# Last down projection: the remainders of the ordinary weight tiles are made by an adding DMA instead of VectorE

## The chip, the core and the metric

The kernel runs on one core of one Trainium2 chip. A core has TensorE (PE, the matrix products), VectorE (DVE, elementwise work), ScalarE (ACT, elementwise work and casts), GpSimd (POOL), SyncE (SP, which here issues the DMAs) and 16 DMA engines that move data between DRAM and the on-chip memory. Each engine works through its own queue in a fixed order and waits at semaphores. The metric is device time in microseconds (us). Before the change the median of three runs is 1831.31 us (1829.83 to 1831.4).

## What is computed

The reference is one transformer block on 256 tokens of width 2048, in float32: a feed-forward half step, a mixer (differential attention beside a causal convolution), and a second feed-forward half step, each with a normalisation, a modulation and a gated residual.

```
x = x + 0.5 * g1 * swiglu(h, ffn1_w_gu, ffn1_w_down)
x = x + gm * hybrid_mixer(h, ...)
x = x + 0.5 * g2 * swiglu(h, ffn2_w_gu, ffn2_w_down)
def swiglu(h, w_gu, w_down):
    g, u = split(h @ w_gu)          # 2048 -> 2 x 5632
    return (silu(g) * u) @ w_down   # 5632 -> 2048
```

The change lies in the very last product, `(silu(g) * u) @ ffn2_w_down`: 256 tokens by 5632 by 2048.

## The kernel before

Float32 accuracy is reached with three products of a faster, rounded type (fp32r). Every operand is split into a rounded part `hi` and a remainder `lo = value - hi`, and `mm3` (L326) adds `a_hi*w_hi` (L329), `a_hi*w_lo` (L333) and `a_lo*w_hi` (L334) into one PSUM accumulator.

Weights come from DRAM in tiles of 1 MB: 128 partitions by 4 pieces of 512 columns. `w_tile` (L288) loads a tile into a `raw` buffer with a DMA that SP issues (L294). Then, for each half of two pieces, ScalarE casts the half into a `whi` buffer (L305) and VectorE subtracts this from `raw` into a `wlo` buffer (L307). The pools are small: `rawp`, `whp` and `wlp` have four buffers each (L89 to L91). A `raw` buffer holds a whole tile, a `whi` or `wlo` buffer half a tile, so that two tiles' halves fit.

The last projection is `down_strassen` (L465). It goes twice (`np_` 0 and 1) over the 22 weight tiles `c` of one half of the output columns. Some tiles, listed in `SEVENS` (L57), are done with seven products in place of eight: tiles 3, 5, 9, 11, 13, 15, 17 in the first pass and 1, 3, 5 and so on to 17 in the second. I call these seven-product tiles. Each of them takes one `raw` buffer (loaded at L542), and is split by a helper (L512 on ScalarE, L513 on VectorE) into `b11`, `b21`/`b22`, `t1`/`t3` and `t4`/`t2`, four `whi` and four `wlo` buffers; sums of its pieces are made on VectorE in between (L547, L549, L550). It issues 7 * 3 = 21 products.

All other tiles are ordinary: they go through `w_tile` at L595 and issue 8 * 3 = 24 products, two token halves by two column halves by two contraction pieces. There are 15 of them in the first pass and 13 in the second, 28 in all. The last two of the second pass (20 and 21) are held: their products come at the very end, one accumulator after the other (L597, and the loop whose inner line is L630), so that each accumulator can be finished and stored while the next is still being summed.

Buffers are shared in order. A tile's cast can start only when the engine that last used that `whi` buffer is done with it, and here that is TensorE, some four half tiles earlier. The order of instructions on each engine's queue was fixed by a planner at build time; a blocked instruction blocks what is behind it on its own engine.

Of the kernel before, what the change touches and what calls it, by code (L numbers as in the profile page):

```python
# [16 lines left out]
F32 = mybir.dt.float32  # L17
F32R = mybir.dt.float32r
# [4 lines left out]
ALU = mybir.AluOpType  # L23
AX = mybir.AxisListType

P = 128
# [56 lines left out]
def block_kernel(ctx: ExitStack, tc: tile.TileContext, x_in, pos_in, w_ada, small, w_gu1, w_dn1,  # L83
                 w_in, w_out, w_gu2, w_dn2, out):
    nc = tc.nc
# [3 lines left out]
    rawp = ctx.enter_context(tc.tile_pool(name="rawp", bufs=4))  # L89
    whp = ctx.enter_context(tc.tile_pool(name="whp", bufs=4))  # L90
# [9 lines left out]
    def nm(s):  # L100
        uid[0] += 1
        return f"{s}_{uid[0]}"

    def blk(shape, dtype=F32):
        return blkp.tile(shape, dtype, tag="blk", name=nm("blk"))
# [7 lines left out]
    def acc_tile(shape=(P, 512)):  # L113
        return accp.tile(list(shape), F32, tag="acc", name=nm("acc"))

    def tp_tile(shape=(P, 512)):
        return tpp.tile(list(shape), F32, tag="tp", name=nm("tp"))
# [26 lines left out]
    for i in range(4):  # L144
        pc = acc_tile()
        for j in range(4):
            k = 4 * i + j
# [138 lines left out]
    w_dma = [None]  # L286

    def w_tile(src, held=False, ks=(0, 4), small_raw=False):  # L288

        k0, n = ks[0], ks[1] - ks[0]  # L290
        src = src.rearrange("p (k n) -> p k n", k=4)
        if not small_raw:
            raw = rawp.tile([P, 4, 512], F32, tag="raw", name=nm("raw"))
            w_dma[0] = nc.sync.dma_start(out=raw[:, :n, :], in_=src[:, k0:k0 + n, :])  # L294
        views = {}
        for h in range(0, n, 2):
            m = min(2, n - h)
            if small_raw:
                part = blk([P, 2, 512])
                w_dma[0] = nc.sync.dma_start(out=part[:, :m, :], in_=src[:, k0 + h:k0 + h + m, :])  # L300
                rw = part[:, :m, :]
            else:
                rw = raw[:, h:h + m, :]
            hi = blk([P, 2, 512], F32R) if held else whp.tile([P, 2, 512], F32R, tag="whi", name=nm("whi"))
            nc.scalar.copy(out=hi[:, :m, :], in_=rw)  # L305
            lo = blk([P, 2, 512], F32R) if held else wlp.tile([P, 2, 512], F32R, tag="wlo", name=nm("wlo"))
            nc.vector.tensor_sub(out=lo[:, :m, :], in0=rw, in1=hi[:, :m, :].bitcast(F32))  # L307
            for j in range(m):
                views[k0 + h + j] = (hi[:, j, :], lo[:, j, :])
        return lambda j: views[j]  # L310

    def w_first(cs, held):

        n = len(cs)
        raw = blk([P, 2, 512])
        w_dma[0] = nc.sync.dma_start(out=raw[:, :n, :], in_=w_gu1[cs[0]:cs[0] + n, 0].rearrange("c p n -> p c n")[:, :, :512])
        hi = blk([P, 2, 512], F32R) if held else whp.tile([P, 2, 512], F32R, tag="whi", name=nm("whi"))
        lo = blk([P, 2, 512], F32R) if held else wlp.tile([P, 2, 512], F32R, tag="wlo", name=nm("wlo"))

        def split():  # L320
            nc.scalar.copy(out=hi[:, :n, :], in_=raw[:, :n, :])  # L321
            nc.vector.tensor_sub(out=lo[:, :n, :], in0=raw[:, :n, :], in1=hi[:, :n, :].bitcast(F32))

        return [lambda j, i=i: (hi[:, i, :], lo[:, i, :]) for i in range(n)], split

    def mm3(acc, a, w, start, stop, lo_last=False):  # L326
        ah, al = a
        wh, wl = w
        nc.tensor.matmul(acc, ah, wh, start=start, stop=False)  # L329
        if lo_last:  # L330
            nc.tensor.matmul(acc, al, wh, start=False, stop=False)
            return nc.tensor.matmul(acc, ah, wl, start=False, stop=stop)
        nc.tensor.matmul(acc, ah, wl, start=False, stop=False)  # L333
        return nc.tensor.matmul(acc, al, wh, start=False, stop=stop)  # L334
# [130 lines left out]
    def down_strassen(w_dn, aT, a_act, gate_of, evac_last, share, pend, finish):  # L465
# [43 lines left out]
        def split(src, n):  # L509
            hi = whp.tile([P, 2, 512], F32R, tag="whi", name=nm("whi"))  # L510
            lo = wlp.tile([P, 2, 512], F32R, tag="wlo", name=nm("wlo"))
            nc.scalar.copy(out=hi[:, :n, :], in_=src)  # L512
            nc.vector.tensor_sub(out=lo[:, :n, :], in0=src, in1=hi[:, :n, :].bitcast(F32))  # L513
            return [(hi[:, i, :], lo[:, i, :]) for i in range(n)]
# [4 lines left out]
        for np_ in range(2):  # L519
# [17 lines left out]
            for c in range(NCH):  # L537
                share()
                first, last = c == 0, c == NCH - 1
                if c in SEVENS[np_]:  # L540
                    raw = rawp.tile([P, 4, 512], F32, tag="raw", name=nm("raw"))
                    nc.sync.dma_start(out=raw, in_=w_dn[np_, c].rearrange("p (k n) -> p k n", k=4))  # L542
                    s1, s2, s3, s4 = sums_of(c)
                    (b11,) = split(raw[:, 0:1, :], 1)
                    b21, b22 = split(raw[:, 2:4, :], 2)

                    nc.vector.tensor_sub(out=raw[:, 0:2, :], in0=raw[:, 1:4:2, :], in1=raw[:, 0:2, :])  # L547
                    t1, t3 = split(raw[:, 0:2, :], 2)
                    nc.vector.tensor_sub(out=raw[:, 3, :], in0=raw[:, 3, :], in1=raw[:, 0, :])  # L549
                    nc.vector.tensor_sub(out=raw[:, 2, :], in0=raw[:, 2, :], in1=raw[:, 3, :])  # L550
                    t4, t2 = split(raw[:, 2:4, :], 2)
                    go, end = c == SEVENS[np_][0], c == SEVENS[np_][-1]
                    if go:
                        if np_ == 0:
                            seven = [acc_tile(), acc_tile(), tp_tile(), tp_tile()]
                        else:
                            seven = [acc_tile() for _ in range(4)]
                    mm3(seven[0], a_act(2 * c, 0), b11, go, end)
                    mm3(plain[0], a_act(2 * c + 1, 0), b21, False, False)
                    mm3(plain[1], s4, b22, False, False)  # L560
                    mm3(seven[1], s1, t1, go, end)
                    mm3(seven[3], s3, t3, go, end)
                    mm3(seven[2], s2, t2, go, end)
                    mm3(plain[2], a_act(2 * c + 1, 1), t4, False, False)
                    tick()
                    if end:

                        p1, p5, p6, p7 = seven
                        u = [tmp([P, 512]) for _ in range(5)]
                        last_pair = np_ == 1  # L570
                        nc.scalar.copy(out=u[0], in_=p1)
                        nc.vector.tensor_add(out=u[4], in0=p6, in1=u[0])

                        def step_1(u=u, p5=p5):
                            nc.vector.tensor_add(out=u[1], in0=p5, in1=u[4])

                        def step_2(u=u, p7=p7):
                            nc.vector.tensor_add(out=u[2], in0=p7, in1=u[4])

                        def step_3(u=u, p5=p5):  # L580
                            nc.vector.tensor_add(out=u[3], in0=p5, in1=u[2])

                        def add(i, u=u):

                            t, n, xs = place(i)
                            nc.vector.tensor_mul(out=u[i], in0=u[i], in1=gbc[n])
                            nc.vector.tensor_add(out=xs, in0=xs, in1=u[i])

                        if last_pair:
                            todo += [lambda: (step_1(), add(0), add(1)), lambda: (step_2(), step_3(), add(2)),  # L590
                                     lambda: add(3)]
                        else:
                            todo += [step_1, step_2, step_3]
                    continue
                w = w_tile(w_dn[np_, c])  # L595
                if np_ == 1 and c >= NCH - 2:
                    held.append((c, w))  # L597
                    if todo:
                        todo.pop(0)()
                    continue  # L600
                for k in range(2):
                    for i, (t, n) in enumerate(order):
                        mm3(plain[i], a_act(2 * c + k, t), w(2 * k + n), first and k == 0, last and k == 1)
                tick()
                if first and np_ == 0:
                    while pend:
                        finish(*pend.pop(0))
                    gbc = gate_of()
                if todo:
                    todo.pop(0)()  # L610
# [691 lines left out]
    for ci in range(10):  # L1302
        p0 = 1 if ci < HOLD else 0
        accs = first[ci][2] if ci < HOLD else [acc_tile() for _ in range(NT)]
        for pc in range(p0, 4):
# [3 lines left out]
            w = w_tile(w_in[ci, pc], ci == 0 and pc <= PRE)  # L1309
# [52 lines left out]
    for i, (n, pc) in enumerate([(n, pc) for pc in range(4) for n in range(3)]):  # L1362
        w = w_tile(w_out[n, pc])
# [106 lines left out]
```

## Time and profile before

| | |
|---|---|
| median of three runs | 1831.31 us |
| the profiled execution's own time | 1830.85 us |
| its span, first to last instruction | 1829.0 us |
| TensorE busy, share of the span | 98% |
| VectorE busy | 84% |
| ScalarE busy | 55% |
| GpSimd busy | 2% |
| mean DMA traffic | 274 GB/s |

The profile is one execution. A row of a timeline gives the start in us from the beginning of the span, the duration in us, the engine, the line of the kernel, the operation, what it writes and reads, a count where equal rows are merged, and in brackets the idle time before it with what ended it. A row of a group gives the count, the total busy time, the mean of one in ns, and the idle time ahead of it. A windows row gives, for one stretch, the busy time and instruction count of PE, weight loading, DVE, ACT and POOL. The last projection runs from about 1580 us to the end at 1829.0 us.

### The profile page before, as it was taken

How to read it: one execution, taken by the hardware profiler on the slowest of the kernel's cores; microseconds unless marked ns; L12 is line 12 of the kernel's file. 1: busy time of each engine (PE TensorE's matmuls, PEld its weight loads, DVE VectorE, ACT ScalarE, POOL GpSimd, SP SyncE). 2: the span in 40 equal slices, each digit the busy share in tenths (PEclk: the TensorE clock that was granted, in tenths of full speed). 3: DMA queues.
4: the chain of work that ended last, by engine and by line, in shares of the span. 5: the costliest groups of instructions: out<-in, count | busy, mean ns of one | idle time of the engine just before them, and what ended most of it. 6: DMA issues, size and time to landing. Idle time of an engine off the chain costs nothing.

```text
span 1829.0 us, 21917 instructions
## 1 busy us (share of the span) xinstructions
PE 1800.7 (98%) x8111; PEld 1480.9 (81%) x8111; DVE 1531.0 (84%) x2040; ACT 1010.5 (55%) x1527; POOL 28.3 (2%) x29
## 2 busy tenths in 40 slices
PE   6999999999999999999999999999999999999998
PEld 5788888888888887788888787888888888878787
DVE  7889869999888787898999778878887865599897
ACT  7554344444444343566798655664755665555453
POOL 0000000000000000000110100000000000000000
PEclk9999999999999999999999999999999999999999
DMA  9987978889889998775544466889898966655552
GB/s 375 359 308 296 349 276 300 336 314 339 338 325 352 352 340 331 285 262 198 184 142 158 174 240 254 324 338 347 278 300 289 328 232 202 218 200 221 184 213 110
DMA packets 95962, 501.68 MB, mean 274 GB/s; under 512 B 31424, under 2 KB 31856, under 8 KB 38384
## 3 DMA queue, kind: packets, MB, share of 16 engines
q1 hardware_dynamic: 95856, 500.30, 74.7%
q8 instruction: 63, 1.03, 0.2%
q14 instruction: 43, 0.35, 0.1%
HBM read 492.37 MB, written 2.12 MB: 270 GB/s over the span
## 4 chain that ended last, share of the span: by engine, by line
PE 85%; DVE 8%; DMA 3%; ACT 3%; issue 2%; POOL 0%; SPq 0%; POOLq 0%; DVEq 0%; ACTq 0%
PE acc L333 27%; PE acc L334 27%; PE acc L329 27%; DVE wlo L307 2%; DVE wlo L513 1%; DMA raw<-in_w_ada_dram 1%; ACT whi L305 1%; DMA blk<-in_w_gu_dram 1%; PE acc L1137 1%; DVE raw L193 1%; DMA tmp<-tmp 1%; DVE blk L1029 1%; PE tp L851 1%; PE tp L333 1%; PE tp L334 1%
## 5 line engine op out<-in xcount | busy, mean ns | idle before, releaser
L333 PE MATMUL acc<-wlo,blk 128*128 128x512 f32 x2336 | 911.8, 390 | 6.3 <-DVE wlo L307 6.3
L329 PE MATMUL acc<-whi,blk 128*128 128x512 f32 x2339 | 909.5, 392 | 2.3 <-ACT blk L403 1.3
L334 PE MATMUL acc<-whi,blk 128*128 128x512 f32 x2336 | 910.7, 390 | 0.0
L305 ACT CAST whi<-raw 128x1024 fp32r<-128x1024 f32 (+1 forms) x577 | 592.4, 1044 | 475.5 <-PE acc L334 328.3
L307 DVE TENSOR_TENSOR wlo<-raw,whi 128x1024 fp32r<-128x1024 f32 (+1 forms) x577 | 686.5, 1210 | 180.3 <-ACT whi L305 179.5
L333 PEld LDWEIGHTS acc<-wlo,blk 128*128 128x128 f32 x2336 | 438.8, 188 | 101.4 <-DVE wlo L307 11.3
L329 PEld LDWEIGHTS acc<-whi,blk 128*128 128x128 f32 x2339 | 438.8, 188 | 94.6 <-ACT whi L305 2.7
L334 PEld LDWEIGHTS acc<-whi,blk 128*128 128x128 f32 x2336 | 438.5, 188 | 91.5 <-DVE blk L405 0.6
L193 DVE CUSTOM_DVE_ANT_0 raw<-raw,c_bc 128x2048 f32<-128x2048 f32 x142 | 324.2, 2285 | 10.3 <-DMA raw<-in_w_ada_dram 10.1
L512 ACT CAST whi<-raw 128x512 fp32r<-128x512 f32 (+1 forms) x64 | 60.5, 946 | 78.2 <-PE acc L334 27.5
L513 DVE TENSOR_TENSOR wlo<-raw,whi 128x512 fp32r<-128x512 f32 (+1 forms) x64 | 69.2, 1086 | 11.6 <-ACT whi L512 11.5
L666 ACT COPY blk<-acc 128x512 f32<-128x512 f32 x72 | 41.9, 589 | 62.6 <-PE acc L334 60.0
L1029 DVE SCALAR_TENSOR_TENSOR blk<-blk,cst,blk 128x245 f32<-128x245 f32 (+21 forms) x176 | 70.4, 455 | 0.6 <-ACT blk L1027 0.5
L830 DVE TENSOR_TENSOR blk<-acc,blk 128x512 f32<-128x512 f32 x88 | 56.7, 682 | 0.1
L845 ACT COPY tmp<-tmp 128x1024 uint16<-128x1024 uint16 x22 | 29.8, 1355 | 45.6 <-DMA tmp<-tmp 45.6
L831 ACT ACTIVATE blk<-blk 128x256 f32<-128x256 f32 x88 | 33.7, 413 | 19.6 <-DVE blk L830 19.4
L329 PE MATMUL acc<-blk,blk 128*128 128x512 f32 x104 | 40.8, 396 | 1.4 <-ACT blk L321 1.4
L333 PE MATMUL acc<-blk,blk 128*128 128x512 f32 x100 | 39.1, 391 | 0.8 <-DVE blk L307 0.8
L334 PE MATMUL acc<-blk,blk 128*128 128x512 f32 x100 | 39.0, 392 | 0.0
L351 DVE TENSOR_TENSOR blk<-tmp,blk 128x512 fp32r<-128x512 f32 x22 | 15.1, 688 | 22.3 <-ACT blk L350 22.3
L832 DVE TENSOR_TENSOR blk<-blk 128x256 f32<-128x256 f32 x88 | 33.8, 417 | 0.0
L307 DVE TENSOR_TENSOR blk<-raw,blk 128x1024 fp32r<-128x1024 f32 x24 | 28.9, 1220 | 2.0 <-ACT blk L305 2.0
(227 smaller groups left out, 1064.4 us busy)
## 6 DMA issues: line engine op xcount, KB each, us to landing
raw<-in_w_gu_dram SPq DMA_DIRECT2D x161, 1024.0 KB, 6.1
raw<-in_w_ada_dram SPq DMA_DIRECT2D x142, 1024.0 KB, 6.7
raw<-in_w_dn_dram SPq DMA_DIRECT2D x88, 1024.0 KB, 5.3
raw<-in_w_in_dram SPq DMA_DIRECT2D x40, 1024.0 KB, 4.8
raw<-in_w_out_dram SPq DMA_DIRECT2D x16, 1024.0 KB, 4.8
raw<-in_w_gu_dram SPq DMA_DIRECT2D x8, 768.0 KB, 6.3
blk<-in_w_gu_dram SPq DMA_DIRECT2D x10, 512.0 KB, 13.7
blk<-gate_line SPq DMA_DIRECT2D x6, 512.0 KB, 4.8
```

What stands on the lines that cost most here:

```text
L193: nc.vector.tensor_tensor_reduce(out=raw, in0=raw, in1=c_bc, scale=1.0, scalar=0.0, op0=ALU.mult, op1=ALU.add, accum_out=ada_cols[g][:, j ...
L305: nc.scalar.copy(out=hi[:, :m, :], in_=rw)
L307: nc.vector.tensor_sub(out=lo[:, :m, :], in0=rw, in1=hi[:, :m, :].bitcast(F32))
L329: nc.tensor.matmul(acc, ah, wh, start=start, stop=False)
L333: nc.tensor.matmul(acc, ah, wl, start=False, stop=False)
L334: return nc.tensor.matmul(acc, al, wh, start=False, stop=stop)
L512: nc.scalar.copy(out=hi[:, :n, :], in_=src)
L513: nc.vector.tensor_sub(out=lo[:, :n, :], in0=src, in1=hi[:, :n, :].bitcast(F32))
L666: last_part[0] = nc.scalar.copy(out=parts[c][:, t, :], in_=accs[t])
L830: nc.vector.tensor_add(out=p[:, t, :], in0=accs[t], in1=p[:, t, :])
L832: nc.vector.tensor_mul(out=p[:, t, 256:], in0=p[:, t, :256], in1=p[:, t, 256:])
L1029: nc.vector.scalar_tensor_tensor(out=y[:, d:], in0=u, scalar=w, in1=y[:, d:], op0=ALU.mult, op1=ALU.add)
```

## The change

The ordinary tiles of the last projection go through a new function, `w_tile_dma`, in place of `w_tile`. It loads the tile into `raw` and casts the halves into `whi` as before. VectorE's subtraction is gone. In its place ScalarE multiplies each rounded half by -1 and writes it into a tile `lo`. When both halves are there, a DMA issued by GpSimd reads the same 1 MB of weight from DRAM a second time and adds it onto `lo`, which leaves `weight - hi`. `lo` is not a `wlo` buffer: it is a whole tile from the pool `rawp`, with the tag `raw`, so it takes one of the four `raw` buffers until the tile's last product.

```diff
+    def w_tile_dma(src):
+
+        src = src.rearrange("p (k n) -> p k n", k=4)
+        raw = rawp.tile([P, 4, 512], F32, tag="raw", name=nm("raw"))
+        w_dma[0] = nc.sync.dma_start(out=raw, in_=src)
+        views = {}
+        lo = rawp.tile([P, 4, 512], F32R, tag="raw", name=nm("raw"))
+        for h in range(0, 4, 2):
+            hi = whp.tile([P, 2, 512], F32R, tag="whi", name=nm("whi"))
+            nc.scalar.copy(out=hi, in_=raw[:, h:h + 2, :])
+            nc.scalar.mul(lo[:, h:h + 2, :], hi.bitcast(F32), -1.0)
+            for j in range(2):
+                views[h + j] = (hi[:, j, :], lo[:, h + j, :])
+        nc.gpsimd.dma_start(out=lo, in_=src, accum_op=ALU.add)
+        return lambda j: views[j]
@@
-                w = w_tile(w_dn[np_, c])
+                w = w_tile_dma(w_dn[np_, c])
```

## The prediction

> **What bounds the kernel now.** I read the page's busy times first, then the stage of the change by windows, then who waits for whom there, and last the timeline of one pair of tiles. The page:
>
> ```profile
> span 1829.0 us, 21917 instructions
> PE 1800.7 (98%) x8111; PEld 1480.9 (81%) x8111; DVE 1531.0 (84%) x2040; ACT 1010.5 (55%) x1527; POOL 28.3 (2%) x29
> ```
>
> TensorE sets the time. Windows of 20 us in the last projection, and its whole from 1580 us, say whether it waits there; the first columns are the stretch, its length, then PE, weight loads, DVE, ACT and POOL:
>
> ```profile
> 1600.00:1620.00 20.00, 19.70 (x87) 15.62 (x86) 19.96 (x33) 10.33 (x13) 0.00 (x0) 1.00 0.49 182
> 1620.00:1640.00 20.00, 19.79 (x87) 16.06 (x88) 19.93 (x33) 11.77 (x14) 0.00 (x0) 1.00 0.55 210
> 1700.00:1720.00 20.00, 19.45 (x84) 15.21 (x84) 17.60 (x23) 8.30 (x9) 0.00 (x0) 1.00 0.42 150
> 1720.00:1740.00 20.00, 18.60 (x79) 14.04 (x78) 19.67 (x28) 10.16 (x12) 0.00 (x0) 1.00 0.52 193
> 1760.00:1780.00 20.00, 20.00 (x90) 16.57 (x89) 17.85 (x19) 11.31 (x12) 0.00 (x0) 1.00 0.57 210
> 1800.00:1820.00 20.00, 19.16 (x84) 15.22 (x83) 17.78 (x24) 6.39 (x7) 0.00 (x0) 1.00 0.19 65
> 1580.00:1829.00 249.00, 241.26 (x1050) 195.45 (x1048) 216.56 (x273) 126.97 (x140) 0.00 (x0) 1.00 0.51 188
> ```
>
> A stretch without waits holds 90 products. The five others shown lack 3, 3, 6, 11 and 6, 29 in all. A product takes its turn every 0.227 us (the rows of 1770.62 and 1770.84 below), so all that TensorE loses in this stage is 29 * 0.227 = 6.6 us. Its waits name VectorE and ScalarE about equally:
>
> ```profile
> PE acc L333 <- DVE wlo L307: 0.8, 2, 0.7
> PE acc L329 <- ACT whi L305: 0.6, 3, 0.2
> PE acc L329 <- ACT whi L512: 0.6, 1, 0.6
> PE acc L333 <- DVE wlo L513: 0.5, 1, 0.5
> ```
>
> So 6.6 us is the most that a lighter VectorE can give back, although it is busy for 216.56 of 249 us. GpSimd does nothing here, so its queue holds nothing that the new DMAs could delay.
>
> **The change, part by part.** Removed: 56 subtractions on VectorE. Added: 56 multiplications on ScalarE, and 28 adding DMAs of 1 MB. The nearest rows:
>
> ```profile
> L307 DVE TENSOR_TENSOR wlo<-raw,whi 128x1024 fp32r<-128x1024 f32 x57 | 68.1, 1219 | 13.6 <-ACT whi L305 13.6
> L305 ACT CAST whi<-raw 128x1024 fp32r<-128x1024 f32 x56 | 57.4, 1050 | 24.3 <-PE acc L334 14.5 <-PE tp L334 7.0 <-DVE tmp L490 1.7
> L836 ACT COPY tmp<-blk 128x1024 uint16<-128x1024 uint16 x10 | 10.4, 1039 | 2.0 <-DVE blk L832 2.0
> ```
>
> VectorE loses 56 * 1.219 = 68 us of work; I credit the change with the whole 6.6 us. ScalarE gains 56 multiplications, which I price as the cast of the same shape, 1.05 us: 59 us more on 126.97 of 249 us, 75% in all, so its total is covered by TensorE's work. What is not covered is its place. The multiplication stands between the cast and the remainder, and the DMA behind it. How early can that chain start? One pair in the second pass, ScalarE, VectorE and TensorE:
>
> ```profile
> 1766.10 1.05 ACT L512 CAST whi<-raw 128x1024 fp32r<-128x1024 f32 x1 [1.66 <-PE tp L334]
> 1767.06 2.15 ACT L305 CAST whi<-raw 128x1024 fp32r<-128x1024 f32 x2
> ...
> 1768.33 2.35 DVE L307 TENSOR_TENSOR wlo<-raw,whi 128x1024 fp32r<-128x1024 f32 x2
> ...
> 1765.63 0.39 PE L334 MATMUL tp<-whi,blk 128*128 128x512 f32 x1
> 1765.86 0.39 PE L329 MATMUL acc<-whi,blk 128*128 128x512 f32 x1
> ...
> 1770.39 0.39 PE L334 MATMUL tp<-whi,blk 128*128 128x512 f32 x1
> 1770.62 0.39 PE L329 MATMUL acc<-whi,blk 128*128 128x512 f32 x1
> 1770.84 0.39 PE L333 MATMUL acc<-wlo,blk 128*128 128x512 f32 x1
> ```
>
> At E = 1765.86 an ordinary tile ends and a seven-product tile begins (21 * 0.227 = 4.76 us, until 1770.62). Its last cast, at 1766.10, had waited for TensorE: it needs the `whi` buffer that the ordinary tile's last product releases. Only behind it come the next ordinary tile's two casts, and VectorE's two remainders end at 1768.33 + 2.35 = 1770.68. TensorE wants the first at 1770.84. The lead is 0.16 us; today there is no room for anything longer, and the `whi` pool, which is unchanged, sets it.
>
> After the change ScalarE does cast, multiplication, cast, multiplication, each 0.96 us behind the last (1767.06 less 1766.10): the last begins at 1769.94 and ends at 1770.99, E + 5.13. Then comes L, the time from there until the added remainder has landed. TensorE meanwhile can do the first product of each of the four accumulators, since an accumulator takes its products in order and the second needs `lo`. The other 20 follow the landing: 20 * 0.227 = 4.54. The next E comes at E + 9.67 + L instead of E + 45 * 0.227 = 10.2. Each ordinary tile behind a seven-product tile costs **L - 0.5**; there are 16 (seven in the first pass, nine in the second).
>
> In a run of ordinary tiles the lead is a tile longer:
>
> ```profile
> 1806.86 1.06 ACT L305 CAST whi<-raw 128x1024 fp32r<-128x1024 f32 x1 [1.67 <-PE tp L334]
> 1809.58 1.05 ACT L305 CAST whi<-raw 128x1024 fp32r<-128x1024 f32 x1 [1.66 <-PE tp L334]
> 1812.30 1.06 ACT L305 CAST whi<-raw 128x1024 fp32r<-128x1024 f32 x1 [1.67 <-PE tp L334]
> ...
> 1806.66 0.39 PE L329 MATMUL acc<-whi,blk 128*128 128x512 f32 x1
> ...
> 1812.10 0.39 PE L329 MATMUL acc<-whi,blk 128*128 128x512 f32 x1
> ```
>
> Tile 18 ends at 1806.66 and frees the second half of tile 20 (cast at 1806.86); its multiplication ends at 1806.86 + 0.96 + 1.05 = 1808.87, 2.21 behind. Tile 20 then ends 2.21 + L + 4.54 after tile 18, against 2 * 5.44 = 10.88: **L - 4.1**. The tile behind it has had the same stall to prepare in and costs nothing. So every second tile of a run pays: 0 and 2, 8, 20, and 0 of the second pass, 5 in all. The held pair: tile 21's multiplication ends at 1812.30 + 2.01 = 1814.31, and its remainder is wanted seven products behind 1812.10, at 1813.69: **L + 0.6**. Sum: 16(L - 0.5) + 5(L - 4.1) + L + 0.6 - 6.6 = 22 L - 34.5.
>
> `lo` also takes `raw` buffers. I cost that at nothing: at E the four hold this tile's `lo`, the two tiles now being split, and the next `lo`; the load that waits for E lands 4.9 us later, and its first cast is due a whole pair later. If that cover went, about 1 us per pair, 16 us, would come on top. SP's loads then queue behind that wait, but only loads of later tiles do.
>
> **L itself** is not in this trace: no DMA here adds, and none comes from GpSimd. The nearest:
>
> ```profile
> raw<-in_w_dn_dram SPq DMA_DIRECT2D x41, 1024.0 KB, 4.9
> out_dram<-xall SPq DMA_DIRECT2D x2, 128.0 KB, 1.9
> blk<-in_w_gu_dram SPq DMA_DIRECT2D x10, 512.0 KB, 13.7
> tmp<-tmp SPq DMA_TRANSPOSE x22, 4.5
> ```
>
> From below, the plain load of the same bytes, 4.9 us. From above, 13.7 us, the slowest load, in the crowd at the start. An adding DMA must fetch both addends, so I double the part that moves: 1.9 us is what a small transfer takes, 4.9 - 1.9 = 3.0 is the moving, and L = 1.9 + 2 * 3.0 = 7.9. Sum: 22 * 7.9 - 34.5 = +139 us on the execution's 1830.85 us, 1970; this execution stands 0.5 under the median, so **1971**. With L = 4.9 the sum is +73 (1905), with 13.7 +267 (2098). Even L = 2 would give +9.5: the change pays only below 34.5 / 22 = 1.6 us, less than that small transfer takes.
>
> The Trainium skill speaks against this change too. "DMA: Bandwidth & Descriptors", section "Anatomy of one DMA — SWDGE (gpsimd) path", puts a DMA from GpSimd at 2.0 us plus the bytes over 436 GB/s, and "Collectives: The Full Stack", "The bandwidth ceiling", says that an add needs two source reads and runs at half a copy's rate. By these, as an estimate, L is 2.0 + 2 * 2.4 = 6.8 and the sum +115 (1946). No run here shows either yet.
>
> **Rivals.** *As quick as a load* (L near 4.9): for it, the transfer is otherwise idle half the time (DMA share 0.51); against it, the double fetch. 1905. *Small pieces:* the adder or GpSimd's issue breaks rows up. The transposes move 256 KB in 4.5 us, a quarter of the bytes; at that pace L = 18 and the sum +362: 2193. For it, that an addition must treat elements; against it, rows of 8 KB that lie in one piece on both sides. *The other side, faster:* the planner lays the casts and the DMA far enough ahead that `lo` lands before 1770.84 in every pair. Then only VectorE's relief is left, 1830.85 - 6.6 + 0.5 = 1825. It decides at the `whi` wait of 1766.10: as long as that stands, it can't be. *Nothing happens:* part of the stalls hidden, the gain eating the rest, 1831; it needs L near 1.6.
>
> **How the numbers follow.** The forecast (L from about 6 to 13.7) has 0.65, as quick as a load 0.16, small pieces 0.12, faster 0.04, nothing 0.03. The range holds the first two: 1890, a little under 1905 for pulled-ahead products that I didn't count, to 2110, a little over 2098. About 0.2 is left out. A measurement here can tell 0.2%, 3.7 us, from no change: faster 0.04, same 0.03, slower 0.93.
>
> **What would show it.** TensorE's waits in this stage name the DMA into `raw` at L333, some 20 times, of 7 us each behind seven-product tiles and under 4 us within runs. GpSimd's 28 DMAs land 7.9 us after issue. VectorE's and ScalarE's busy times there change by -68 and +59 us, and nothing changes before 1580 us. I am wrong if `lo` lands early: then either the planner freed `whi` sooner, or L is far below a plain load.

## The result and the profile after

The changed kernel takes 2042.44 us (2041.59 to 2045.55, four runs), against 1831.36 us (1829.83 to 1832.42, four runs) for the kernel before on the same chip. The ratio is 1.1156 [1.1137, 1.1176]: 211 us slower. The forecast was 1971, 139 us slower. The time lies inside the range, but the loss is half as large again as forecast.

The page of the profile after (line numbers are 16 higher than before, so that the three products are now L345, L349 and L350, the cast is L321, the multiplication L322 and the adding DMA L325):

```profile
span 2040.0 us, 22048 instructions
PE 1862.1 (91%) x8111; PEld 1516.8 (74%) x8111; DVE 1471.4 (72%) x1984; ACT 1069.1 (52%) x1583; POOL 53.2 (3%) x57
PEclk8999999999999999999999999999999877787877
```

The windows of the kernel after, the last 20 us ahead of the stage and the stage itself:

```profile
1560.00:1580.00 20.00, 20.00 (x90) 16.57 (x89) 11.17 (x13) 11.24 (x13) 0.00 (x0) 1.00 0.41 120
1580.00:2040.00 460.00, 300.56 (x1044) 229.07 (x1042) 155.64 (x216) 183.57 (x196) 24.88 (x28) 0.79 0.62 169
```

Up to 1580 us nothing has changed: the window ahead holds 90 products, like an undisturbed one before. The whole loss lies in the last projection, which takes 460 us in place of 249. Two things are to be read there. TensorE is busy in only 300.56 of 460 us, so it waits. And its busy time has itself grown, from 241.26 to 300.56 us, with practically the same number of products, while the granted clock (the column after the busy times) fell from 1.00 to 0.79. VectorE's work fell by 61 us and ScalarE's rose by 57.

Who waits for whom in that stage (engine, tile and line, what was waited for; us in total, times, longest):

```profile
PE acc L349 <- DMA raw<-in_w_dn_dram: 142.1, 23, 9.0
...
PE acc L345 <- ACT whi L528: 7.4, 13, 1.6
...
PE acc L349 <- DVE wlo L529: 5.2, 13, 2.0
```

TensorE waits above all for one thing, the landing of the added remainder, 23 times. The DMA issues of the stage (count, size, median us from issue to landing) show the plain loads on SP's queue and the adding ones on GpSimd's:

```profile
raw<-in_w_dn_dram SPq DMA_DIRECT2D x42, 1024.0 KB, 5.1
raw<-in_w_dn_dram POOLq DMA_DIRECT2D x28, 1024.0 KB, 8.3
```

One pair of the second pass as a timeline. An ordinary tile ends at 1927.18 (call it E), 18 products of a seven-product tile start from there to 1931.05 (its first three were done before E), and the next ordinary tile follows; first ScalarE, then GpSimd, then TensorE:

```profile
1927.38 1.05 ACT L321 CAST whi<-raw 128x1024 fp32r<-128x1024 f32 x1 [2.70 <-PE tp L350]
1928.47 1.06 ACT L322 ACTIVATE raw<-whi 128x1024 fp32r<-128x1024 f32 x1
1929.43 1.04 ACT L321 CAST whi<-raw 128x1024 fp32r<-128x1024 f32 x1
1930.50 1.06 ACT L322 ACTIVATE raw<-whi 128x1024 fp32r<-128x1024 f32 x1
...
1931.97 0.88 POOL L325 DMA_DIRECT2D raw<-in_w_dn_dram  x1 [19.11 <-ACT raw L322]
...
1931.28 0.61 PE L345 MATMUL acc<-whi,blk 128*128 128x512 f32 x2
1931.73 0.61 PE L345 MATMUL tp<-whi,blk 128*128 128x512 f32 x2
...
1940.10 0.80 PE L349 MATMUL acc<-raw,blk 128*128 128x512 f32 x1 [5.95 <-DMA raw<-in_w_dn_dram]
1940.69 0.63 PE L350 MATMUL acc<-whi,blk 128*128 128x512 f32 x1
1941.12 0.63 PE L349 MATMUL acc<-raw,blk 128*128 128x512 f32 x1
...
1946.16 0.40 PE L345 MATMUL tp<-whi,blk 128*128 128x512 f32 x1
1946.39 0.40 PE L349 MATMUL tp<-raw,blk 128*128 128x512 f32 x1
```

The chain is there as forecast: the first cast waits for the `whi` buffer that TensorE frees at E, four instructions run one behind the other until 1930.50 + 1.06 = 1931.56, the DMA goes out at 1931.97, and TensorE, after four products that don't need `lo` and the first three of the next seven-product tile (until 1934.15, between small waits for that tile's split), stands still until 1940.10. What the prediction doesn't have is seen after that: the products then start 0.43 us apart (1940.69, 1941.12) for five and a half microseconds, and only from 1946.16 again 0.23 us apart. The granted clock, read by windows, is 0.50 from 1935.80 to 1946.04 and 1.00 on either side. The pair takes 20.4 us in place of 10.2.

The starts of all products in the stage close the account. TensorE has 26 waits of over 1.2 us, 152 us together. 213 products start at 0.38 to 0.5 us, mostly 0.427, after the one ahead, which is 42 us over the regular 0.227. Another 23 us are left: some 10 are again products at half clock (the next one starts 0.56 to 0.59 us behind the first after a wait), and some 13 are small waits, mostly for the split of seven-product tiles. Before, small waits were 6 us and the rest was nil. 152 + 42 + 23 - 6 = 211 us, the whole difference. So the loss has two main parts, **the waits** and **slow products behind the waits**.

### The profile page after: what moved, and what is told of

Same layout as the page of the kernel before. It is cut to its first block, busy times and chain, and to the rows that moved or that the text cites. A ratio compares the mean times of both kernels' runs of the same rounds, so it can differ in the third digit from the quotient of the medians.

```text
span 2040.0 us, 22048 instructions
## 1 busy us (share of the span) xinstructions
PE 1862.1 (91%) x8111; PEld 1516.8 (74%) x8111; DVE 1471.4 (72%) x1984; ACT 1069.1 (52%) x1583; POOL 53.2 (3%) x57
## 3 DMA queue, kind: packets, MB, share of 16 engines
q0 software_dynamic: 4032, 29.36, 7.4%
## 4 chain that ended last, share of the span: by engine, by line
PE 72%; issue 19%; DVE 4%; DMA 3%; ACT 2%; POOL 0%; POOLq 0%; DVEq 0%; SPq 0%; ACTq 0%
PE acc L349 23%; PE acc L350 23%; PE acc L345 23%; DMA raw<-in_w_dn_dram 2%; DVE wlo L307 1%; DMA xall<-in_x_dram 1%; PE acc L1153 1%; DVE blk L1045 0%; PE tp L867 0%; PE tp L410 0%; ACT whi L305 0%; DVE raw L193 0%; DVE blk L307 0%; DMA tmp<-tmp 0%; DVE tmp L420 0%
## 5 line engine op out<-in xcount | busy, mean ns | idle before, releaser
L350 PE MATMUL acc<-whi,blk 128*128 128x512 f32 x2336 | 930.7, 398 | 0.1
L345 PE MATMUL acc<-whi,blk 128*128 128x512 f32 x2339 | 910.0, 395 | 9.0 <-ACT whi L528 7.4
L349 PE MATMUL acc<-wlo,blk 128*128 128x512 f32 x2164 | 846.4, 391 | 10.1 <-DVE wlo L529 5.2
L305 ACT CAST whi<-raw 128x1024 fp32r<-128x1024 f32 x521 | 536.1, 1044 | 463.8 <-PE acc L350 330.2
L307 DVE TENSOR_TENSOR wlo<-raw,whi 128x1024 fp32r<-128x1024 f32 x521 | 620.4, 1210 | 175.7 <-ACT whi L305 174.7
L345 PEld LDWEIGHTS acc<-whi,blk 128*128 128x128 f32 x2339 | 444.4, 190 | 107.1 <-ACT whi L528 12.9
L350 PEld LDWEIGHTS acc<-whi,blk 128*128 128x128 f32 x2336 | 452.0, 194 | 94.8 <-DVE blk L421 0.7
L349 PEld LDWEIGHTS acc<-wlo,blk 128*128 128x128 f32 x2164 | 406.6, 188 | 101.1 <-DVE wlo L529 9.8
L349 PE MATMUL acc<-raw,blk 128*128 128x512 f32 x172 | 92.3, 536 | 142.1 <-DMA raw<-in_w_dn_dram 142.1
L349 PEld LDWEIGHTS acc<-raw,blk 128*128 128x128 f32 x172 | 45.0, 262 | 162.4 <-DMA raw<-in_w_dn_dram 103.2
L321 ACT CAST whi<-raw 128x1024 fp32r<-128x1024 f32 x56 | 58.0, 1046 | 86.2 <-PE acc L350 51.4
L322 ACT ACTIVATE raw<-whi 128x1024 fp32r<-128x1024 f32 x56 | 58.5, 1057 | 1.2
L325 POOL DMA_DIRECT2D raw<-in_w_dn_dram x28 | 24.9, 889 | 882.9 <-ACT raw L322 834.9
L345 PE MATMUL acc<-blk,blk 128*128 128x512 f32 x104 | 41.2, 399 | 1.4 <-ACT blk L337 1.4
L847 ACT ACTIVATE blk<-blk 128x256 f32<-128x256 f32 x88 | 33.3, 412 | 12.9 <-DVE blk L846 12.9
```

Source lines behind the costliest of these rows:

```text
L321: nc.scalar.copy(out=hi, in_=raw[:, h:h + 2, :])
L322: nc.scalar.mul(lo[:, h:h + 2, :], hi.bitcast(F32), -1.0)
```

## The experiments

My theory was this: the chain (buffer freed at E, two casts and two multiplications, adding DMA) sets the waits, and the pause in each wait is what makes the products behind it slow. The rivals: the second read of the weights itself, or the `raw` buffers that `lo` takes, hold the stage up; and the slow products come from something that the adding DMAs do, not from the pause. In all of these kernels line numbers differ by a few. The kernel before took 1829.8 to 1831.2 us beside them. A time without a ratio beside it is that of one execution.

**A second load without the chain.** The remainder is left out: GpSimd copies the weight a second time into `lo`, at the start of the tile, with no negation and no addition, so that `lo` holds the weight itself.

```diff
+        nc.gpsimd.dma_start(out=lo, in_=src)
         for h in range(0, 4, 2):
-            nc.scalar.mul(lo[:, h:h + 2, :], hi.bitcast(F32), -1.0)
-        nc.gpsimd.dma_start(out=lo, in_=src, accum_op=ALU.add)
```

> The second DMA stays on GpSimd and still fills a whole raw buffer with 1 MB, but it only copies the weight and waits for nothing that ScalarE does; the negations are gone. (The remainder is left out: the weight itself stands in its place.) Theory, chain: the loss is the remainder that lands late behind cast, negation and DMA, 146 us of waiting, and slow products after each wait, 64 us. Without the chain the same traffic and buffers cost little: 1825 to 1850. Rival, buffers and traffic: a second megabyte per tile and raw buffers held until the last product starve the loads; then most of the loss stays, above 1930.

It took 1841.74 us. The stage's window:

```profile
1580.00:1840.00 260.00, 244.53 (x1044) 194.70 (x1042) 154.17 (x216) 125.03 (x140) 14.13 (x27) 0.99 0.80 292
```

The same 29 MB are read a second time, the same `raw` buffers are taken, and the stage is only 11 us longer, at a granted clock of 0.99. Neither the bytes nor the buffers make the 211 us as long as the chain is absent. (These bytes are copied; what adding them costs the DMA engines comes further below.)

**The chain without the addition.** Everything stays, but the DMA overwrites instead of adding (so the remainder is again left out).

```diff
-        nc.gpsimd.dma_start(out=lo, in_=src, accum_op=ALU.add)
+        nc.gpsimd.dma_start(out=lo, in_=src)
```

> As changed, cast, negation and then the DMA from GpSimd, but this DMA copies the weight over the negated tile and adds nothing. (The remainder is left out.) It prices the addition. If the double fetch is dear, landing falls from 8.3 us to about 5.5 after issue, each of some 22 waits shortens by 3 us, and the time is about 1975. If the dear part is GpSimd's issue and not the addition, landing stays near 8 us and the time near 2040.

It took 1975.17 us, as expected. Its issues:

```profile
raw<-in_w_dn_dram SPq DMA_DIRECT2D x42, 1024.0 KB, 4.8
raw<-in_w_dn_dram POOLq DMA_DIRECT2D x28, 1024.0 KB, 5.3
```

A copy from GpSimd's queue lands in 5.3 us, half a microsecond behind a load from SP's. The addition makes it 8.3: it costs 3.0 us, and issuing from GpSimd costs half a microsecond. (In the run before, with more loads beside them, the same copies landed in 7.3 us.) Two thirds of the loss (145 of 211 us) would be there with a plain copy too. Its waits are shorter (22, of some 3 to 4 us), yet 185 products still ran slow, 37 us.

**Only behind seven-product tiles, and only elsewhere.** The two kinds of places of the prediction, one at a time.

```diff
-                w = w_tile_dma(w_dn[np_, c])
+                w = (w_tile_dma if c - 1 in SEVENS[np_] else w_tile)(w_dn[np_, c])
```

> The change only on the 16 ordinary tiles directly behind a seven-product tile; the other 12 go the old way. By the prediction's account these carry 16 of the 22 delays of full length. A pair takes 20.4 us where it took 10.2, so 16 * 10.2 = 163 of the 211 us: about 1994. Rival: if every adding DMA costs the same, 16 of 28, the loss is 121: 1952.

```diff
-                w = w_tile_dma(w_dn[np_, c])
+                w = (w_tile if c - 1 in SEVENS[np_] else w_tile_dma)(w_dn[np_, c])
```

> The change only on the other 12 tiles: the runs of ordinary tiles at the start, middle and end of a pass, and the held pair. By the prediction's account the rest of the 211 us, 48: about 1879. Rival, every adding DMA costs the same, 12 of 28: 90 us, 1921.

They took 1998.69 us (169 us over the kernel before; expected 1994) and 1897.65 us (68 over; between the two theories' 1879 and 1921, so that this one decides nothing). Together they lose some 26 us more than the whole change does, so the parts don't simply add up: the first has 16 waits for the remainder with 106.1 us, the second 8 with 52.0, which is 158 us against 142.1 when both are changed. Which neighbours make up the difference was not traced.

**The pause filled with products of zero.** To tell whether the pause makes the products slow, TensorE gets something to do in it. Behind each seven-product tile the four first products are issued and then 24 products with a zero operand, which add nothing. One buffer that is kept elsewhere is given to the zeros.

```diff
+FILL = 6
-KEPT = 6
+KEPT = 5
...
+                after_seven = c > 0 and c - 1 in SEVENS[np_]
+                if after_seven:
+                    for i, (t, n) in enumerate(order):
+                        nc.tensor.matmul(plain[i], a_act(2 * c, t)[0], w(n)[0], start=False, stop=False)
+                    for _ in range(FILL):
+                        for i, (t, n) in enumerate(order):
+                            nc.tensor.matmul(plain[i], zero, w(n)[0], start=False, stop=False)
```

> As changed, and in each of the 16 ordinary tiles behind a seven-product tile, after the first product of each accumulator, 24 more products with a stationary operand of zeros, which add nothing: 384 products of 0.227 us, 87 us of work more. (One set of sums is worked out twice to make room.) Theory, idle: the 13 to 14 products after a wait take 0.427 us in place of 0.227 because TensorE had stood idle; the zero products fill 5.4 of some 5.8 us, the wait shrinks by what they take, and the slow products become quick: 16 * 14 * 0.2 = 45 us faster than the changed kernel, about 2000. Rival, contention: they are slow because the adding DMA or the loads occupy the memory; then they stay slow and the time stays at 2040 or above.

It took 2043.26 us: the total didn't move, and that expectation was missed. In the trace the slow products fell from 213 to 156, the waits of over 1.2 us from 152 to 93 us and the rest from 23 to 6, some 87 us less in all. But 16 * 24 * 0.227 = 87 us of zero products were put in. The planner also set the seven-product tile's last cast ahead of the chain again, so that the remainder landed about 1 us later behind E (13.9 us at 1939.95, against 12.9 in the pair above). The pauses that were left behind most seven-product tiles, 2.3 to 3.0 us, came out on either side. TensorE behind two of them:

```profile
1939.95 0.47 PE L631 MATMUL acc<-raw,blk 128*128 128x512 f32 x1 [2.65 <-DMA raw<-in_w_dn_dram]
1940.26 0.39 PE L632 MATMUL acc<-whi,blk 128*128 128x512 f32 x1
1940.49 0.40 PE L631 MATMUL acc<-raw,blk 128*128 128x512 f32 x1
...
1958.70 0.70 PE L631 MATMUL acc<-raw,blk 128*128 128x512 f32 x1 [2.83 <-DMA raw<-in_w_dn_dram]
1959.19 0.63 PE L632 MATMUL acc<-whi,blk 128*128 128x512 f32 x1
1959.62 0.63 PE L631 MATMUL acc<-raw,blk 128*128 128x512 f32 x1
```

The same products, on the same buffers, are 0.23 us apart behind one pause and 0.43 behind the other. The granted clock tells the two apart. In all traces of this study it changes only on a grid of 3.413 us. The stretches of that grid around the two pauses (the last three columns: granted clock, DMA share, GB/s):

```profile
1934.89:1938.30 3.41, 2.42 (x11) 1.68 (x9) 1.51 (x3) 0.00 (x0) 0.00 (x0) 1.00 1.06 221
1938.30:1941.71 3.41, 1.76 (x8) 1.48 (x9) 0.00 (x0) 0.00 (x0) 0.00 (x0) 1.00 0.19 38
1955.37:1958.78 3.41, 0.58 (x4) 0.19 (x3) 0.00 (x0) 0.00 (x0) 0.00 (x0) 1.00 0.71 144
1958.78:1962.19 3.41, 3.41 (x9) 2.67 (x10) 0.00 (x0) 0.00 (x0) 0.00 (x0) 0.50 0.00 0
```

The first pause lies across two stretches, 1.16 us of it in one and 1.65 in the other (counted from 0.227 us behind the last product's start). The second, 2.99 us counted so, lies in one, and the stretch behind it runs at half clock, while the DMA engines stand idle (share 0.00): no transfer can slow it there. So the next run filled the rest of the pause, with 36 zero products for each tile.

```diff
-FILL = 6
+FILL = 9
```

> As the run with 24 zero products, but 36: 192 more products, 44 us more of work, which close the 2.3 to 2.9 us that were left of most waits. Theory, idle: waits shorter than 2.3 us were followed by no slow product in any run so far, longer ones by 7 to 16; with the wait closed the slow products behind these 16 tiles vanish, about 1.4 us each, and the time falls by some 10 to 25 us against the run with 24, to 2018 to 2033. Rival, contention: slow products stay or the time grows, 2043 or more.

It took 2024.9 us, as expected: with 192 products more than the last kernel, it was 18 us faster. (That expectation's remark that no wait under 2.3 us had brought slow products was wrong: in the run with the chain but no addition and in the one with late remainder products some had, as the table below counts.)

```profile
1580.00:2023.00 443.00, 390.83 (x1637) 313.90 (x1635) 160.64 (x224) 183.26 (x200) 24.82 (x28) 0.95 0.66 177
```

The granted clock of the stage is 0.95, and the slow products are down to 60 (12 us). The adding DMAs are all still there, and the DMA share is higher (0.66) than in the changed kernel. Contention with them would have kept the products slow. It is the pause that makes them so.

All the traces of this study together (the kernel before, the kernel after and the twelve experiments; waits of TensorE in the last projection, and how many of them were followed, before the next wait, by at least five products of about 0.427 us):

| wait, us | waits | followed by slow products | slow products, mean |
|---|---|---|---|
| 1.2 to 2.5 | 70 | 14 | 1.9 |
| 2.5 to 3.0 | 21 | 17 | 6.1 |
| 3.0 to 4.5 | 31 | 25 | 7.1 |
| over 4.5 | 93 | 89 | 8.4 |

From about 2.5 us on, a wait usually brings slow products, six to eight on average (13 in the pair of the changed kernel above), and its length matters little. What decides is the idle time within one stretch of the grid, short waits added up. I worked it out for every stretch of the 14 traces from the starts of the products, 0.227 us for each (0.427 at half clock). Of the stretches at full clock, 147 had half clock in the next one, and they were idle for 2.05 us or more; the other 991 were idle for at most 2.10 us. The clock came back behind each stretch at half clock with less than 0.77 us idle, and behind none with more than 0.92.

**More `whi` buffers.** The prediction puts the start of the chain down to the `whi` pool. Here the ordinary tiles' rounded halves get buffers of their own, taken from those that are otherwise kept.

```diff
-KEPT = 6
+KEPT = 2
...
-            hi = whp.tile([P, 2, 512], F32R, tag="whi", name=nm("whi"))
+            hi = blk([P, 2, 512], F32R)
```

> As changed, but the rounded halves of the ordinary tiles get four buffers of their own, so that their casts no longer wait for the seven-product tiles' buffers (to make room, four sets of sums are not kept but worked out again in the second pass). Theory, the whi buffers set when the chain starts: the cast can follow the raw load, about 6 us after the pair before has ended; the next pair is then limited by load, casts, negations and DMA in a row, about 12 us in place of 20.4; waits fall under 2 us a pair and the products after them stay quick: about 1880. Rival, the raw buffers or the DMA's own rate set it: little changes, above 2000.

It took 1958.71 us, against some 1880 expected. The loss fell from 211 to 128 us, so the `whi` pool was indeed the first limit. The rest did not go, because the next limit came up at once:

```profile
PE acc L349 <- DMA raw<-in_w_dn_dram: 88.5, 18, 9.1
...
ACT blk L321 <- DMA raw<-in_w_dn_dram: 49.0, 13, 12.7
ACT whi L528 <- DMA raw<-in_w_dn_dram: 34.5, 13, 10.4
```

Now ScalarE's casts wait for the plain loads (49.0 us and 34.5 us, against 5.9 and 10.1 in the changed kernel), and a pair takes about 15 us. The added remainder lands 10.3 us after its issue, no longer 8.3.

**The remainder's products one tile later.** The products with `lo` are issued behind the next tile's, which gives the chain a tile more of time; `whi` is kept longer for it.

```diff
+                ws = [w(j) for j in range(4)]
                 for k in range(2):
                     for i, (t, n) in enumerate(order):
-                        mm3(plain[i], a_act(2 * c + k, t), w(2 * k + n), first and k == 0, last and k == 1)
+                        a, (wh, wl) = a_act(2 * c + k, t), ws[2 * k + n]
+                        nc.tensor.matmul(plain[i], a[0], wh, start=first and k == 0, stop=False)
+                        last_mm[0] = nc.tensor.matmul(plain[i], a[1], wh, start=False, stop=False)
+                if late:
+                    late.pop()()
...
+                                nc.tensor.matmul(plain[i], a_act(2 * c + k, t)[0], ws[2 * k + n][1], start=False,
+                                                 stop=last and k == 1)
```

> As changed, but the eight products of a tile that need the remainder are issued one tile later, behind the next tile's products; the 16 others, which release the rounded halves, go first. Nothing is left out. The remainder then has a tile's time more, 3.6 + 4.8 us, about what it takes to land. Theory, chain: the waits nearly vanish and with them the slow products: 1825 to 1860. Rival, buffers: the remainder now holds its raw buffer for a tile longer, the loads start late, and much of the loss stays: above 1930.

It took 1940.69 us, far from the 1825 to 1860 expected. TensorE's waits for the remainder are nearly gone (15.0 us over seven waits, and one of 8.3), and pairs take 13.6 us. TensorE now waits for ScalarE's split of the seven-product tile, and ScalarE's casts for the loads:

```profile
ACT whi L528 <- DMA raw<-in_w_dn_dram: 45.8, 13, 15.2
...
ACT whi L321 <- DMA raw<-in_w_dn_dram: 36.4, 6, 13.8
...
PE acc L345 <- ACT whi L528: 31.2, 27, 5.0
```

In the changed kernel these casts waited 16 us for loads, in the kernel before not at all. The loads land late here for two reasons that this run doesn't separate: they take longer (7.2 us in the median, 5.1 in the changed kernel), and they may start late, for want of a free `raw` buffer. The next runs take `lo` out of `raw`.

**Halves in buffers of their own.** `lo` moves out of `raw` into two half buffers, each with its own DMA of 512 KB, first in the old order of products and then in the late one.

```diff
-KEPT = 6
+KEPT = 2
...
-        lo = rawp.tile([P, 4, 512], F32R, tag="raw", name=nm("raw"))
         for h in range(0, 4, 2):
-            nc.scalar.mul(lo[:, h:h + 2, :], hi.bitcast(F32), -1.0)
+            lo = blk([P, 2, 512], F32R)
+            nc.scalar.mul(lo, hi.bitcast(F32), -1.0)
-        nc.gpsimd.dma_start(out=lo, in_=src, accum_op=ALU.add)
+            nc.gpsimd.dma_start(out=lo, in_=src[:, h:h + 2, :], accum_op=ALU.add)
```

> The changed kernel with only the second of the two steps: remainder halves in buffers of their own, a DMA of 512 KB for each, products in the old order. (Four sets of sums are worked out again.) Theory: the whi buffers still set the start, so TensorE still waits for both halves; but the first DMA starts 2 us earlier and each moves half: the second lands about 6 us after its negation in place of 8.5, and 12 products follow it in place of 20: some 4 to 5 us less of 20.4 a pair, 1950 to 1985. Rival, the raw buffers made the loss: below 1860.

> As the run with the late remainder products, but the remainder halves have four buffers of their own in place of raw buffers, each filled by its own adding DMA of 512 KB (four sets of sums are worked out again to make room). Nothing is left out. There the loads into the raw buffers had become the bound, 13.6 us a pair. Theory, chain first and raw buffers second: with both gone a pair takes 10.2 us again, TensorE hardly waits, and VectorE's relief is left: 1822 to 1840. Rival, DMA: adding DMAs and loads together can't be moved in 10.2 us a pair, and it stays above 1880.

In the old order it took 1993.83 us, 49 us better than the change but above the 1950 to 1985 expected. The chain from E still stands, half the bytes in each DMA landed no earlier than the whole (8.7 us), and TensorE waited 104.0 us for them, at 29 places. In the late order it took 1892.68 us, ratio 1.0338 [1.0321, 1.0355] against the kernel before. The loads there take longer still (8.5 us in the median), and yet no cast waits for one any more: this speaks for their late start, and so for the four `raw` buffers, as what held the run with the late products. The kernel is still 62 us slower than the one before, far from the 1822 to 1840 expected. TensorE's waits for the remainder, 30.3 us in 20, are the largest single item of that. The rival named in its expectation, the DMA engines, fits. Windows of this kernel (the column before the last is the mean busy share of the 16 DMA engines, the last GB/s):

```profile
1660.00:1720.00 60.00, 54.70 (x237) 43.80 (x235) 35.88 (x50) 43.52 (x48) 10.55 (x12) 0.99 1.01 293
1720.00:1744.00 24.00, 19.18 (x61) 14.11 (x62) 5.04 (x6) 8.85 (x9) 5.29 (x6) 0.78 1.05 260
1788.00:1836.00 48.00, 43.56 (x181) 32.95 (x181) 33.42 (x48) 31.48 (x37) 7.03 (x8) 1.00 0.97 261
1580.00:1892.00 312.00, 263.41 (x1050) 201.64 (x1048) 163.45 (x241) 179.34 (x200) 49.45 (x56) 0.93 0.91 244
```

In three of these four stretches the DMA engines are full or nearly so, in two of them at 260 GB/s, a rate that plain transfers passed with the share at 0.80 (292 GB/s in the first experiment). The two queues of the whole stage (packets, MB, share of the 16 engines) say why:

```profile
q0 software_dynamic: 8064, 29.36, 49.3%
q1 hardware_dynamic: 9095, 46.54, 41.5%
```

The adding DMAs (q0) move 29.36 MB in 49.3% of the time, the loads 46.54 MB in 41.5%: an added byte takes 1.9 times the DMA engines' time of a loaded one. It is the addition and not GpSimd's queue: where that queue only copied (the chain without the addition), 29.36 MB took 20.6% and the loads' 48.43 MB 33.9%, the same for each byte. In the run of ordinary tiles from 1720 to 1744 us, where TensorE is busy for 19.18 of 24 us, its only waits are for adding DMAs (8.6 us). The rest of the 62 us was not divided up.

**Only a few tiles.** The last question was whether a few such tiles, late order and all, pay at all: four of them, and two.

```diff
+ADD = ((0, 4), (0, 6), (1, 2), (1, 4))
...
-                w = w_tile_dma(w_dn[np_, c])
+                w = (w_tile_dma if (np_, c) in ADD else w_tile)(w_dn[np_, c])
```

> The kernel of before, with the adding DMA only at four ordinary tiles behind seven-product tiles in the stretches where VectorE is full (tiles 4 and 6 of the first pass, 2 and 4 of the second), and there with the remainder's products issued one tile later. Nothing is left out. Theory: one adding DMA a pair, spaced out, lands in the time that the late products give it, and TensorE gets back part of the 6.6 us that it lost to a full VectorE: 1826 to 1830 against 1830 before. Rival: the chain of four tiles is not covered, each costs some us: 1835 to 1850.

```diff
-ADD = ((0, 4), (0, 6), (1, 2), (1, 4))
+ADD = ((0, 4), (1, 2))
```

> As the run with four tiles, with two (tile 4 of the first pass and 2 of the second). Theory: half the relief, 1828 to 1831. Rival, uncovered chain: 1832 to 1840.

Four took 1849.82 us, ratio 1.0111 [1.0096, 1.0127]; two took 1839.14 us, ratio 1.0053 [1.0041, 1.0066]. Both came out with the rival: 4 to 5 us lost for each adding DMA, though the DMA engines are far from full (a share of 0.53 to 0.56) and TensorE hardly waits for the remainder (2.7 us with four, not at all with two). With two, TensorE's waits name the next seven-product tile's casts:

```profile
PE acc L346 <- ACT whi L529: 2.9, 4, 1.2
PE acc L350 <- DVE wlo L530: 2.2, 2, 2.0
```

These are waits at ScalarE's and VectorE's split of the seven-product tile. A load beside an adding DMA landed up to 12.7 us after its issue there, against 7.7 at most in this stage before. With two, some 4 of the 9 us lost are again products at half clock (17 of them 0.427 us apart). Whether the late loads, the two multiplications or the changed order of the queues make the waits was not separated and stays open. None of the versions beat the kernel before, which had only 6.6 us to gain.

## Why the prediction was right and wrong

**The direction and the chain were right.** No room for anything longer than the subtraction, the start at the `whi` buffer freed at E, the four products ahead of the wait: the timeline shows each. The buffer set the start: with `whi` buffers of their own 84 us of the loss went. The chain's end was put at E + 5.13; it is E + 4.38 (1931.56), because the planner took the seven-product tile's last cast out of its way.

**L was nearly right, and its working held.** 7.9 us forecast; 8.3 measured from the issue (8.5 from the multiplication's end, 1931.56, to TensorE's start, 1940.10). The added part was worked out as a second moving time of 3.0 us, and copy against addition measured 3.0. By the Trainium skill's two pages the estimate was 6.8, 1.7 too little from the multiplication's end. Its rule that an add needs two source reads ("Collectives: The Full Stack", "The bandwidth ceiling", there for a collective reduction) agrees in size: 1.9 times the engines' time for a byte here, beside a ratio of 1.93 on that page. The traces show the time, not the reads.

**The sum of the waits was right, but partly since errors cancelled.** Forecast 22 * 7.9 - 27.9 = 146 us of waits for the remainder; the profile has 142.1 in 23 waits. By places it differs. Those behind seven-product tiles are mostly 5.3 to 6.2 us (1940.10: 5.95), not 7.4. In the pair shown the remainder comes at E + 12.9, as forecast (5.13 + 7.9 = 13.0): the chain ends earlier and L is longer. It is the wait that begins later, at E + 7.0 and not E + 5.7, because three of the products ahead of it are the next seven-product tile's and come late, behind small waits for their split. The five in runs are 34.5 us together, 5 to 9 each, not 19; "under 4 us within runs" was wrong.

**What was put at nothing cost little, for a reason that had an end.** The `raw` buffers held little up in the changed kernel: ScalarE's casts waited 16 us in all for loads. That cover was the slow chain itself; once TensorE no longer waited for the chain (the late order), the casts waited 82 us for loads, and none once `lo` had buffers of its own. VectorE's relief, forecast at 68 us of work, is 61 in the windows and could give back its 6.6 us at most.

**The term that was missing** stands in the step "The other 20 follow the landing: 20 * 0.227 = 4.54." In this trace products behind a wait don't start 0.227 us apart. In the pair shown they need 1947.55 - 1940.10 = 7.45 us for the 20, where 1947.55 is the next E. Over the stage that is 42 us in 213 products, and some 10 of the other 23. The prediction took the clock of 1.00 in the windows before as given; but there TensorE had no pause over 1.2 us, so that row could say nothing about a kernel with pauses of 6 us. Forecast were 146 - 7 = 139 us, measured 211: of the 72 between them some 52 are this term, and the rest are waits, most of them small, that the prediction didn't count.

The Trainium skill has this rule, "TensorE: Matmul & The Clock Gate", Part 1, and the prediction left it out: a TensorE that stands idle for a window of 3.4 us falls to half its clock, with 426.7 ns from start to start for 512 columns. The 0.427 us here agrees. The pause that suffices is shorter here than the "no PE-idle gaps >~3.4µs" of that page's "HAM oscillation": 17 of 21 waits between 2.5 and 3.0 us were enough, and so was idle time of more than 2.1 us within one stretch of 3.41 us.

Of the rivals, none came true. The copy, which lands nearly as quickly as a load, took 1975 us, not the 1905 of "as quick as a load": most of the difference is the same missing term.

## What to carry to other kernels

Price a stall on TensorE twice: the wait, and the products behind it at half pace, here one to three microseconds for most waits of over 2.5 us; a kernel without pauses shows nothing of this in its profile. Before an engine's operation is replaced by a longer chain, look for the release that starts it and count the slack from there (0.16 us here): a cheaper engine is no gain when there is no slack. Moving arithmetic into a DMA is not free on the DMA side either; count the added bytes about twice, and look which loads stand beside them.

## What I had not expected of the hardware

- TensorE's clock is granted in stretches of 3.413 us on a fixed grid. More than 2.1 us idle in one of them, in one pause or several, was always followed by a stretch at half clock (products 0.427 us apart in place of 0.227), less than 2.05 us never, in 14 traces. So of two pauses nearly as long, 2.65 and 2.83 us, one was followed by slow products and the other not.
- More work can take less time: 192 zero products more, put into the pauses, made the kernel 18 us faster (2043.26 to 2024.9 us), with the granted clock up from 0.89 to 0.95.
- The DMA engines were full at 260 GB/s with adding DMAs among the loads, where loads and copies alone moved 292 GB/s at a share of 0.80.
- One adding DMA at a time already costs 4 to 5 us of this kernel, and plain loads beside it landed up to 12.7 us after issue (7.7 at most before).
